# Ten matmuls over zeros behind the weights' transposes of a 3x3 convolution

## The chip, the cores and the metric

The kernel runs on one core of a Trainium2 chip. The metric is the device time of one execution in microseconds (us), the time of the slowest core, and here there is only one. Before the change three runs took 126.99, 127.69 and 127.93 us, median 127.69 us. One more execution was recorded by the hardware profiler; all durations below come from that one.

## The reference

A 3x3 convolution with padding 1 and stride 1, over 16 images with 64 input channels of 64 x 64 and 128 output channels, all in float32:

```
x_pad = np.pad(x, ((0, 0), (0, 0), (1, 1), (1, 1)))
for b, co, ci, kh, kw:
    output[b, co] += weight[co, ci, kh, kw] * x_pad[b, ci, kh:kh+h, kw:kw+w]
```

The input is 16 x 64 x 64 x 64 numbers (16.8 MB), the output 16 x 128 x 64 x 64 (33.6 MB).

## The kernel before

**Arithmetic.** The rows of an output are made in pairs, by a one-dimensional trick in the vertical direction. For output rows 2j and 2j+1 the kernel forms the sum of input rows 2j and 2j+1 (tile `ss`, line 68) and multiplies it by the middle row of weights; this product `U` serves both output rows. The even row is `U` plus a product `A` of two more input rows with the weights G21 and G0, the odd row is `U` plus a product `B` with G01 and G2. G21 and G01 are differences of rows of weights, made on GpSimd (lines 87 and 88). So a block needs 5 products by 3 horizontal taps instead of 6 by 3.

**Tiling.** Two images lie side by side on the 128 partitions (64 channels each). There are 8 such pairs `p`, and each is done in 4 blocks of 8 row pairs. A block issues 30 matmuls on TensorE (line 141): 6 for `U`, 12 for `A`, 12 for `B`. They alternate between the two images, which lie in different halves of the array, so that two of them run side by side; below, "a pair of matmuls" is such a pair. Each has a weight load of its own. The products are accumulated in PSUM, from a pool of 8 banks (`psum`, tag `acc`), and a block takes six of them. ScalarE copies the two `U` tiles out to SBUF (`ut`, line 155); VectorE adds `A` and `ut` (line 165), then `B` and `ut` (line 168), and writes the float32 output tile `ot`.

**Start.** SyncE issues the load of the weights (line 42), of the first pair of images `x0` (line 45) and of the pairs 1 to 3 (`xf`, line 49), all in float32. GpSimd casts the weights to float16 (line 53). TensorE transposes them with 18 matmuls against an identity (line 85), three tiles `wp` of the same PSUM pool, and ScalarE copies these out as `Wt` (line 86). When `x0` has landed, VectorE makes the four pieces of `ss` of pair 0 (line 68) and ScalarE casts `x0` to float16 in four pieces (line 92). The first matmul of line 141 waits for the first of VectorE's pieces. Pairs 4 to 7 come later through GpSimd's queue, cast on the way by the DMA (line 59).

**Stores.** The output of a pair is 4.2 MB in two halves, one for each image: `ots[0]` leaves through SyncE's queue and `ots[1]` through ScalarE's (line 97), both when the fourth block of the pair is done. The last pair is stored in two portions, after its second and its fourth block. Eight buffers are shared by the first loads and the output tiles (`opool`), two of them per pair.

**Order.** Instructions wrapped in `keep` stay in program order on their engine; the others are placed by the framework's scheduler. Each engine runs its own list in order, and waits are semaphores between the lists.

Of the kernel before, what the change touches and what calls it, by code (L numbers as in the profile page):

```python
# [8 lines left out]
F32 = mybir.dt.float32  # L9
F16 = mybir.dt.float16  # L10
# [3 lines left out]
def kernel(  # L14
# [6 lines left out]
    nc = tc.nc  # L21
    B, CI, H, W = x.shape
    CO = weight.shape[0]
# [4 lines left out]
    keep = tc.keep_in_program_order  # L28
# [4 lines left out]
    const = ctx.enter_context(tc.tile_pool(name="const", bufs=1))  # L33
    psum = ctx.enter_context(tc.tile_pool(name="psum", bufs=8, space=bass.MemoryType.PSUM))
# [12 lines left out]
    for p in (1, 2, 3):  # L47
        xf[p] = opool.tile([128, H, W], F32, tag="ot", name="xf")
        nc.sync.dma_start(xf[p], x_rows[128 * p : 128 * p + 128, :, :])
    ident = const.tile([128, 128], F16)  # L50
    make_identity(nc, ident)
    w16 = const.tile([CO, CI * 9], F16)
# [24 lines left out]
    def wrow(i):  # L77
        return Wt[:, i, :, :].rearrange("p t c -> p (t c)")

    for kh, g in ((1, G1), (2, G2), (0, G0)):  # L80
        wp = psum.tile([128, 512], F32, tag="acc", name="wp")
        for k in range(3):
            t = 3 * kh + k
            for q in (0, 64):
                nc.tensor.matmul(wp[q : q + 64, k * CO : k * CO + CO], w16[:, t::9], ident)  # L85
        keep(nc.scalar.copy(wrow(g), wp[:, 0 : 3 * CO]))  # L86
    keep(nc.gpsimd.tensor_sub(wrow(G21), wrow(G2), wrow(G1)))  # L87
    keep(nc.gpsimd.tensor_sub(wrow(G01), wrow(G0), wrow(G1)))  # L88
    load(4)
# [12 lines left out]
    for p in range(NP):  # L102
# [8 lines left out]
        for blk in range(4):  # L111
# [45 lines left out]
            if p + 1 in xf:  # L157
                q = p + 1
# [47 lines left out]
```

## Time and profile before

| what | value |
|---|---|
| median of three runs | 127.69 us |
| the profiled execution | 128.37 us |
| its span, first to last instruction | 126.6 us |
| TensorE busy | 105.8 us (84%), 978 matmuls |
| VectorE, ScalarE, GpSimd busy | 82.7, 52.0, 36.2 us |
| HBM read and written | 17.07 MB and 33.55 MB, 400 GB/s over the span |
| transposes of the weights (line 85) | 4.31 to 5.62 us |
| first and last matmul of line 141 | 9.55 and about 112.8 us |
| last store issued | 115.38 us |

How to read the profile: an engine's busy time says how long its instructions ran, not whether anybody waited for them. The chain of waits goes back from the last computing instruction to what released it, step by step. A transfer is issued by a queue (SPq is SyncE's, ACTq ScalarE's, POOLq GpSimd's) and carried by 16 DMA engines; the "DMA share" of a stretch is the mean busy share of these 16, so 0.50 can mean that eight of them worked all the time; since packets are counted at their start, single short stretches can show a little over 1. "us to landing" counts from the issue of a transfer until the last of the engines is done with it. The column PEclk gives the clock granted to TensorE; the record begins with its first change of state, and before that the column shows 1.00.

The profiled execution took 128.37 us, 1.77 us more than its span (start and end of the program), and 0.68 us more than the median of the runs.

### The profile page before, as it was taken

The page shows a single profiled execution, that of the slowest core. Times are in us where ns is not written, and L with a number is a line of the kernel's source. Part 1 is how long each engine was busy: PE and PEld are TensorE (multiplying, and loading weights), DVE is VectorE, ACT ScalarE, POOL GpSimd, SP SyncE. Part 2 cuts the span into 40 slices and gives each one's busy share as a digit, 9 for nine tenths or more (in the row PEclk, how much of TensorE's full clock was granted, in tenths as well). Part 3 has the DMA queues.
Part 4 walks back from the last instruction along what each step waited for, and adds up shares of the span by engine and source line. Part 5 has one row for each costly group of instructions (what it writes and reads, how often), then busy time and mean ns, then how long its engine had stood idle before and what let it go on. Part 6 is the DMA issues. An engine that isn't in the chain of part 4 may idle for free.

```text
span 126.6 us, 2416 instructions
## 1 busy us (share of the span) xinstructions
PE 105.8 (84%) x978; PEld 57.2 (45%) x978; DVE 82.7 (65%) x132; ACT 52.0 (41%) x84; POOL 36.2 (29%) x27
## 2 busy tenths in 40 slices
PE   0409999999999999999999999999999999990000
PEld 0304455555555555555555555555555555540000
DVE  0025777787778777877777778777877787774000
ACT  4329429933993399333333333333333333330000
POOL 2360093197996000940066000750000000000000
PEclk9999999999999999999999999999999999999855
DMA  6899999999999999999999999999999979999970
GB/s 171 352 456 394 295 306 363 430 440 430 391 324 290 362 396 334 347 321 375 368 352 362 303 409 419 430 419 425 435 430 425 399 316 425 414 438 414 417 324 21
DMA packets 3898, 46.57 MB, mean 368 GB/s; under 512 B 432, under 2 KB 432, under 8 KB 560
## 3 DMA queue, kind: packets, MB, share of 16 engines
q1 hardware_dynamic: 2016, 25.46, 48.2%
q10 hardware_dynamic: 1296, 16.78, 31.5%
q0 software_dynamic: 576, 4.19, 15.8%
q8 instruction: 7, 0.11, 0.3%
q14 instruction: 3, 0.02, 0.0%
HBM read 17.07 MB, written 33.55 MB: 400 GB/s over the span
## 4 chain that ended last, share of the span: by engine, by line
PE 82%; DMA 6%; DVE 2%; issue 1%; DVEq 0%; SPq 0%
PE acc L141 82%; DMA x<-in_x_dram 6%; DVE ot L165 1%; DVE ss L68 1%; DVE ot L168 0%; DVEq L201 0%; SPq L42 0%; DVEq L165 0%
## 5 line engine op out<-in xcount | busy, mean ns | idle before, releaser
L141 PE MATMUL acc<-xs,Wt 64*128 64x504 f16 (+3 forms) x768 | 88.8, 377 | 0.0
L141 PEld LDWEIGHTS <-Wt 64*128 64x128 f16 x960 | 56.1, 95 | 52.0 <-issue 6.0
L165 DVE TENSOR_TENSOR ot<-acc,ut 128x512 f32<-128x512 f32 x64 | 41.2, 686 | 23.8 <-PE acc L141 21.5
L155 ACT COPY ut<-acc 128x512 f32<-128x512 f32 x64 | 34.4, 589 | 54.3 <-issue 34.3
L168 DVE TENSOR_TENSOR ot<-acc,ut 128x512 f32<-128x512 f32 x64 | 41.1, 684 | 0.0
L141 PE MATMUL acc<-ss,Wt 64*128 64x504 f16 (+1 forms) x192 | 27.2, 384 | 3.9 <-DVE ss L68 3.9
L68 POOL TENSOR_TENSOR ss<-xs 128x1024 f16<-128x1024 f16 x8 | 16.8, 2127 | 20.4 <-DMA xs<-in_x_dram 20.4
L68 POOL TENSOR_TENSOR ss<-xf 128x1024 f16<-128x1024 f32 x6 | 14.0, 2355 | 12.5 <-DMA xf<-in_x_dram 12.5
L160 ACT CAST xs<-xf 128x1024 f16<-128x1024 f32 x12 | 12.0, 1057 | 0.0
L68 DVE TENSOR_TENSOR ss<-x 128x512 f16<-128x512 f32 x4 | 2.5, 685 | 8.8 <-DMA x<-in_x_dram 8.8
L59 POOL DMA_DIRECT2D xs<-in_x_dram x4 | 2.4, 601 | 10.4 <-ACT xs L160 10.4
L92 ACT CAST xs<-x 128x1024 f16<-128x1024 f32 (+2 forms) x4 | 3.9, 1042 | 2.6 <-DMA x<-in_x_dram 2.6
L85 PE MATMUL wp<-ident,w 128*64 128x128 f16 x18 | 1.3, 328 | 4.3 <-POOL w L53 4.3
L85 PEld LDWEIGHTS <-w 128*64 128x64 f16 x18 | 1.1, 209 | 4.3 <-POOL w L53 4.3
L86 ACT CAST Wt<-wp 128x384 f16<-128x384 f32 x3 | 1.2, 487 | 3.0 <-PE wp L85 3.0
L86 ACT ACT_TABLE_LOAD x1 | 1.3, 1283 | 0.7 <-PEq L190 0.7
L87 POOL TENSOR_TENSOR Wt<-Wt 128x384 f16<-128x384 f16 x1 | 0.9, 910 | 1.7 <-ACT Wt L86 1.7
L53 POOL CAST w<-w_raw 128x576 f16<-128x576 f32 x1 | 0.7, 664 | 2.3 <-DMA w_raw<-in_weight_dram 2.3
L88 POOL TENSOR_TENSOR Wt<-Wt 128x384 f16<-128x384 f16 x1 | 0.9, 910 | 0.0
masks.py:199 POOL TENSOR_SCALAR_AFFINE_SELECT ident<-ident 128x128 f16<-128x128 f16 x1 | 0.3, 294 | 0.1
masks.py:197 POOL MEMSET ident<- 128x128 f16 x1 | 0.2, 205 | 0.3 <-POOLq L190 0.3
L190 POOL MEMSET const-float32-0.0<- 128x1 f32 x1 | 0.1, 99 | 0.2 <-issue 0.2
(3 smaller groups left out, 0.3 us busy)
## 6 DMA issues: line engine op xcount, KB each, us to landing
out_dram<-ot SPq DMA_DIRECT2D x7, 2048.0 KB, 20.0
out_dram<-ot ACTq DMA_DIRECT2D x7, 2048.0 KB, 19.6
xf<-in_x_dram SPq DMA_DIRECT2D x3, 2048.0 KB, 22.6
xs<-in_x_dram POOLq DMA_DIRECT2D x4, 1024.0 KB, 24.2
x<-in_x_dram SPq DMA_DIRECT2D x1, 2048.0 KB, 7.6
out_dram<-ot SPq DMA_DIRECT2D x2, 1024.0 KB, 11.3
out_dram<-ot ACTq DMA_DIRECT2D x2, 1024.0 KB, 11.2
w_raw<-in_weight_dram SPq DMA_DIRECT2D x1, 288.0 KB, 2.8
```

The source lines that it names most:

```text
L59: keep(nc.gpsimd.dma_start(xs[p], x_rows[128 * p : 128 * p + 128, :, :]))
L68: eng.tensor_add(ss[p][:, lo : lo + n, :], v[:, lo : lo + n, 0, :], v[:, lo : lo + n, 1, :])
L85: nc.tensor.matmul(wp[q : q + 64, k * CO : k * CO + CO], w16[:, t::9], ident)
L86: keep(nc.scalar.copy(wrow(g), wp[:, 0 : 3 * CO]))
L87: keep(nc.gpsimd.tensor_sub(wrow(G21), wrow(G2), wrow(G1)))
L88: keep(nc.gpsimd.tensor_sub(wrow(G01), wrow(G0), wrow(G1)))
L92: keep(nc.scalar.copy(xs[0][:, lo:hi, :], x0[:, lo:hi, :]))
L141: nc.tensor.matmul(tiles[b2][:, lo - j0 : hi - j0, c_lo:c_hi], Wt[p0 : p0 + 64, wi, kw, :], rhs, start=i == 0, stop=i == n - 1,)
L155: keep(nc.scalar.copy(ut, U[b2]))
L160: keep(nc.scalar.copy(xs[q][:, lo : lo + 16, :], xf[q][:, lo : lo + 16, :]))
L165: nc.vector.tensor_add(ots[b2][:, j0 : j0 + RB, 0, :], A[b2], us[b2])
L168: nc.vector.tensor_add(ots[b2][:, j0 : j0 + RB, 1, :], Bt[b2], us[b2])
```

## The change

VectorE first fills a new tile `zeros` (128 x 512, float16) with zeros, and a further tile `warm` is taken from the PSUM pool ahead of the three `wp`. The 18 transposes are now kept in program order, and behind the last of them TensorE runs ten matmuls with 128 columns of `zeros` as weights and all 512 columns as the moving operand, each writing `warm`. Nothing reads `warm`. The first matmul of line 141 comes behind them on TensorE.

```diff
@@ -47,6 +47,14 @@
+    zeros = const.tile([128, 512], F16)
+    keep(nc.vector.memset(zeros, 0.0))
+    warm = psum.tile([128, 512], F32, tag="acc", name="warm")
+
+    def spin(n):
+        for _ in range(n):
+            keep(nc.tensor.matmul(warm, zeros[:, 0:128], zeros))
+
     ident = const.tile([128, 128], F16)
     make_identity(nc, ident)
@@ -82,8 +90,9 @@
             for q in (0, 64):
-                nc.tensor.matmul(wp[q : q + 64, k * CO : k * CO + CO], w16[:, t::9], ident)
+                keep(nc.tensor.matmul(wp[q : q + 64, k * CO : k * CO + CO], w16[:, t::9], ident))
         keep(nc.scalar.copy(wrow(g), wp[:, 0 : 3 * CO]))
+    spin(10)
     keep(nc.gpsimd.tensor_sub(wrow(G21), wrow(G2), wrow(G1)))
```

In the built program the lists of ScalarE, GpSimd and SyncE are the same as before. VectorE's has the memset as a new first instruction. TensorE's has ten weight loads and ten matmuls more, between the transposes and the first matmul of line 141; the first of them waits for the memset. From there on the order on TensorE is that of before, with the PSUM banks shifted by one, so that three of the 192 accumulations of the kernel wait on other semaphores than before; all three lie in the first three blocks.

## The prediction

> **What bounds the kernel now.** I read the chain of waits first. Its pieces in order of time:
>
> ```profile
> 1.17 7.60 DMA x<-in_x_dram
> 9.55 103.26 PE acc L141 x948
> 114.75 0.60 DVE ot L168
> ```
>
> From 9.55 us TensorE runs without a gap to 112.81 us, so it looks like the bound. But this chain stops with VectorE at 115.35 us, and the span is 126.6 us. The last 11 us are transfers, and they have to be read by themselves. The queues on the page:
>
> ```profile
> q1 hardware_dynamic: 2016, 25.46, 48.2%
> q10 hardware_dynamic: 1296, 16.78, 31.5%
> q0 software_dynamic: 576, 4.19, 15.8%
> q8 instruction: 7, 0.11, 0.3%
> ```
>
> The last column adds up to 95.8% of 16 engines' span: 121.3 of 126.6 us. There are 5.3 us in which an average DMA engine did nothing. Where they lie, by stretches of the span (the last two columns are DMA share and GB/s):
>
> ```profile
> 0.00:2.00 2.00, 0.00 (x0) 0.00 (x0) 0.00 (x0) 1.27 (x1) 0.70 (x6) 1.00 0.14 23
> 2.00:101.00 99.00, 92.77 (x858) 50.39 (x860) 71.16 (x114) 46.45 (x76) 35.54 (x21) 1.00 1.01 381
> 101.00:102.50 1.50, 1.50 (x18) 0.81 (x15) 1.50 (x3) 0.60 (x2) 0.00 (x0) 1.00 0.39 164
> 102.50:122.50 20.00, 11.50 (x108) 6.03 (x104) 10.08 (x17) 3.69 (x7) 0.00 (x0) 0.91 0.99 420
> 122.50:125.00 2.50, 0.00 (x0) 0.00 (x0) 0.00 (x0) 0.00 (x0) 0.00 (x0) 0.50 0.14 59
> ```
>
> The DMA engines are full from 2 us to 122.5 us, except for 1.5 us around 101 to 102.5, and there the share is 0.39, not 0: about 6 of 16 worked on. After 122.5 it is 0.14, about 2 of 16. So a few engines lag behind the others, and the end is theirs. Whether the laggards ever run dry is told by the stores. These are the issues of ScalarE's half (column 1 is the time of issue):
>
> ```profile
> 89.77 0.34 ACTq L97 DMA_DIRECT2D out_dram<-ot  x1
> 102.58 0.34 ACTq L97 DMA_DIRECT2D out_dram<-ot  x1
> 108.93 0.34 ACTq L97 DMA_DIRECT2D out_dram<-ot  x1
> 115.38 0.34 ACTq L97 DMA_DIRECT2D out_dram<-ot  x1
> ```
>
> The DMA view, asked for a short stretch around each issue, gives the us to landing for those four in turn:
>
> ```profile
> out_dram<-ot ACTq DMA_DIRECT2D x1, 2048.0 KB, 16.5
> out_dram<-ot ACTq DMA_DIRECT2D x1, 2048.0 KB, 13.6
> out_dram<-ot ACTq DMA_DIRECT2D x1, 1024.0 KB, 12.2
> out_dram<-ot ACTq DMA_DIRECT2D x1, 1024.0 KB, 10.2
> ```
>
> They land at 106.3, 116.2, 121.1 and 125.6 us. The distances are 9.9 us for 4.2 MB (both queues), 4.9 and 4.5 us for 2.1 MB each, while TensorE issued them 12.8, 6.35 and 6.45 us apart. So the last engine ends each store at its own even pace, at 4.9 us per 2.1 MB, and each store is issued long before the one ahead of it has landed (by 3.7, 7.3 and 5.7 us). The earlier ones stand the same way: issued 12.8 us apart, they take 18.5 to 24.5 us to land. **The end of this kernel is set by the DMA engine that lags most, and it has work without a break.** TensorE's end has 5.7 us of cover behind it.
>
> [...]
>
> **The change part by part.** The rows at the start, weight loads of line 141 (start, busy time, count):
>
> ```profile
> 9.93 0.17 PEld L141 LDWEIGHTS <-Wt 64*128 64x128 f16 x2 [0.25 <-issue]
> 10.36 0.18 PEld L141 LDWEIGHTS <-Wt 64*128 64x128 f16 x2 [0.25 <-issue]
> 12.81 0.17 PEld L141 LDWEIGHTS <-Wt 64*128 64x128 f16 x2 [0.20 <-issue]
> 13.18 6.86 PEld L141 LDWEIGHTS <-Wt 64*128 64x128 f16 x64 [0.20 <-issue]
> ```
>
> Up to 13.18 us a pair of matmuls takes 0.43 us at full width (0.375 for the narrower ones); from there 64 loads, 32 pairs, take 6.86 us, 0.214 each. TensorE begins at half pace, and nine pairs take 3.63 us instead of 9 x 0.214 = 1.93: **1.70 us** lost. The granted clock shows 1.00 there, but its record has no entry yet; the pace decides.
>
> *The ten matmuls.* They can begin at 5.62 us (transposes 4.31 plus 1.31). The nearest row is a full-width pair at half pace, 0.43 us: 10 x 0.43 = 4.3 us, end at 9.92, which is **0.37 us** after the 9.55 at which the first real matmul began. Lower end: the pace doubles at once, 10 x 0.214 = 2.1 us, end at 7.8, no delay. Upper end: every load of 128 columns by 128 rows stands beside nothing and costs a transpose's mean of 0.209 on top: 6.4 us, end at 12.0, a delay of 2.45.
>
> *What they gain.* At most the 1.70 us, if the pace is full when the real work begins; at least nothing, if zeros, or this length, do not wake the clock. Before, the pace doubled after 3.6 us of work. From 5.62 that is 9.2, from 4.31 earlier still, so I take all of it: TensorE's work ends 1.70 - 0.37 = 1.33 us earlier. Bounds: 1.70 earlier to 2.45 later.
>
> [...]
>
> *The rest.* The memset lies in VectorE's first 8.80 us, in which it waits for `x0`; behind it only line 68 is queued, and nobody waits unless it took 8 us. Keeping the transposes in order costs nothing, they are in that order already. The shifted banks: block 0 and the next `U` use eight; the next `A` needs the two that ScalarE frees with `ut`, at 12.59 plus 0.53 and 1.06. ScalarE cannot start those earlier, its casts of line 92 run from 8.80 to 12.68. TensorE would reach that `A` at 9.92 + 18 x 0.214 = 13.77, after 13.65: no wait, but that is what is late next, so about 0.1 us of front is left there.
>
> *Where the 1.33 us goes.* All stores are issued 1.33 us earlier. Engines that ran dry near 102 us lose that gap (1.5 us x 0.61 = 0.92 us) and end about 0.9 us earlier. The laggard had no gap: its stores wait 1.33 us longer in the queue and land when they did. Small change: its last 2.1 MB went in 4.5 instead of 4.9 us while the others were out for some 2.8 us; with 0.9 us more of that, 0.4 x 0.9 / 2.8 = 0.13 us. Sum: 128.37 - 0.13 = 128.24 for the profiled execution; that one stands 0.68 over the median, so in runs 127.69 - 0.13 = **127.6 us**. That is no change: about 1% is what a measurement of this kernel can tell from none.
>
> **The rivals.**
> 1. *The lag is not in every execution, the average engine sets the end.* For: the gap at 101 to 102.5 is real, and lag might come and go. Against: eight stores in a row show it. Gain 0.92: 126.8 us.
> 2. *TensorE sets the end after all.* For: it never pauses, and the chain names it. Against: 5.7 us of cover. Gain 1.33 to 1.70: 126.4 to 126.0 us.
> 3. *Slower: the laggard gets one more packet of instructions.* The page shows 7 of them, 0.11 MB, 0.3% of 16 engines' span: 6.1 us, 0.87 us each. If the 20 added instructions push the program over a boundary and the laggard carries the packet: 127.69 + 0.87 = 128.6 us. It decides once the program exceeds what 7 packets and the first fill bring. Against: 20 of 2416 instructions are 0.06 of a packet (0.11 MB / 2416 x 20 = 0.9 KB of 16 KB).
> 4. *It doesn't do what it says*: the clock stays low, the zeros only stand in the way, 0.37 to 2.45 us. All of that lies under the cover, which is at least 10.2 - 7.6 = 2.6 us (a last store of 2.1 MB in both halves against the load of `x0`, the same bytes with almost nothing ahead, 7.6 us): 127.7 us.
>
> **How the numbers follow.** My forecast 0.70 together with rival 4 (both no change, 126.9 to 128.3 by the spread of the runs, 0.94 us, laid around 127.6 and widened to 1.4), rival 1 0.14, rival 2 0.09, rival 3 0.07. Range 126.4 to 128.5: it holds the first two and most of the third, leaves out the lower part of rival 2. Faster by over 1% (under 126.4): rival 2 and a little of 1, 0.10. Slower by over 1% (over 129.0): rival 3 with a bad spread, 0.05. Within 1%: 0.85.
>
> **What would show it.** Right: the slow pairs between 9.9 and 13.2 are gone, the first matmul of line 141 starts at 9.6 to 9.9, the last store is issued near 114 us, the share around 101 us stays near 1, and us to landing of the last stores grows by about 1.3 (10.2 to 11.5) with the span at 126 to 127. Wrong: landing times that do not grow while the issues come earlier (then the engines were not full and rival 1 or 2 holds), or stores that land evenly on all engines.

## The result, and the profile after

The change makes the kernel a little faster: median 126.56 us against 127.93 us, 21 executions each, ratio 0.991 (95% interval 0.989 to 0.994), so 0.9% or about 1.1 us. The ratio, here and below, leaves out executions over 1.5% above the fastest of their kernel, so it can differ from that of the two medians, which are 1.37 us apart here. The forecast was 127.6 us, a gain of 0.13 us. The measured time lies in the range and within the 1% that was called no change, but the gain is eight times the forecast one. It lies between rival 1 (0.92 us) and rival 2 (1.33 us and more), so the size alone does not decide between these.

The start of TensorE's list after the change (start, busy time, count):

```profile
4.30 1.31 PE L93 MATMUL wp<-ident,w 128*64 128x128 f16 x18 [4.30 <-POOL w L61]
5.55 4.44 PE L56 MATMUL warm<-zeros 128*128 128x512 f16 x10
9.92 0.82 PE L150 MATMUL acc<-ss,Wt 64*128 64x512 f16 x6
```

and the weight loads of the real work (line 150 is line 141 of before):

```profile
9.92 9.97 PEld L150 LDWEIGHTS <-Wt 64*128 64x128 f16 x96 [0.83 <-issue]
```

The first real matmul starts at 9.92 us, as worked out (5.62 + 4.3), and the pairs at half pace are gone: 96 loads, 48 pairs, take 9.97 us, 0.208 each, from the first one on. The stores of ScalarE's half, and below them the us to landing of the same four:

```profile
88.34 0.34 ACTq L106 DMA_DIRECT2D out_dram<-ot  x1
101.14 0.34 ACTq L106 DMA_DIRECT2D out_dram<-ot  x1
107.50 0.34 ACTq L106 DMA_DIRECT2D out_dram<-ot  x1
113.95 0.34 ACTq L106 DMA_DIRECT2D out_dram<-ot  x1
```

```profile
out_dram<-ot ACTq DMA_DIRECT2D x1, 2048.0 KB, 15.6
out_dram<-ot ACTq DMA_DIRECT2D x1, 2048.0 KB, 13.5
out_dram<-ot ACTq DMA_DIRECT2D x1, 1024.0 KB, 12.0
out_dram<-ot ACTq DMA_DIRECT2D x1, 1024.0 KB, 9.9
```

All four are issued 1.43 us earlier than before (115.38 to 113.95 for the last), close to the 1.33 of the forecast. But they do not wait longer: 9.9 us instead of 10.2, where 11.5 was forecast. They land at 103.9, 114.6, 119.5 and 123.85 us, the last one 1.75 us earlier than before. The span went from 126.6 to 124.8 us.

Where the DMA engines' time went. These are stretches of the span (last two columns DMA share and GB/s), of the kernel before:

```profile
100.00:106.00 6.00, 6.00 (x60) 3.35 (x58) 5.01 (x8) 2.00 (x4) 0.00 (x0) 1.00 0.85 360
118.00:120.50 2.50, 0.00 (x0) 0.00 (x0) 0.00 (x0) 0.00 (x0) 0.00 (x0) 0.72 1.00 423
120.50:122.00 1.50, 0.00 (x0) 0.00 (x0) 0.00 (x0) 0.00 (x0) 0.00 (x0) 0.50 1.04 437
122.00:125.50 3.50, 0.00 (x0) 0.00 (x0) 0.00 (x0) 0.00 (x0) 0.00 (x0) 0.50 0.21 87
```

and after:

```profile
100.00:106.00 6.00, 6.00 (x60) 2.75 (x58) 4.69 (x8) 2.15 (x4) 0.00 (x0) 1.00 1.01 429
118.00:120.50 2.50, 0.00 (x0) 0.00 (x0) 0.00 (x0) 0.00 (x0) 0.00 (x0) 0.50 1.02 433
120.50:122.00 1.50, 0.00 (x0) 0.00 (x0) 0.00 (x0) 0.00 (x0) 0.00 (x0) 0.50 0.84 355
122.00:125.50 3.50, 0.00 (x0) 0.00 (x0) 0.00 (x0) 0.00 (x0) 0.00 (x0) 0.50 0.09 37
```

The dry stretch at 100 to 106 us is gone: 6 x 0.15 = 0.90 us of an average engine before, nothing after. Beside it, the **idle tail**, what an average engine idles between 118 us and the last landing, has become shorter. Before it is 125.6 - 118 = 7.6 us less the busy 2.5 x 1.00 + 1.5 x 1.04 + 3.5 x 0.21 = 4.8: 2.8 us. After it is 5.85 less 4.13: 1.7 us. Together 2.0 us, against 1.75 of the last landing; the packets themselves took 0.4 us more of an average engine (97.5% of 124.8 us against 95.8% of 126.6), which takes the rest. So two things ended sooner: a common dry stretch, and the lag of the last engines, of which the forecast had said that it would stay. Whether the second belongs to the change is not shown by this: one profiled execution stands on each side, and that of before was a long one (128.37 us).

### The profile page after: what moved, and what is told of

The parts are those of the page before. It is cut to its first block, busy times and chain, and to the rows that moved or that the text cites. A ratio compares the mean times of both kernels' runs of the same rounds, so it can differ in the third digit from the quotient of the medians.

```text
span 124.8 us, 2437 instructions
## 1 busy us (share of the span) xinstructions
PE 108.2 (87%) x988; PEld 49.3 (40%) x988; DVE 82.8 (66%) x133; ACT 52.0 (42%) x84; POOL 36.2 (29%) x27
## 4 chain that ended last, share of the span: by engine, by line
PE 86%; DMA 2%; DVE 1%; issue 1%; POOL 1%; DVEq 0%
PE acc L150 81%; PE warm L56 4%; DMA w_raw<-in_weight_dram 2%; PE wp L93 1%; DVE ot L174 1%; POOL w L61 1%; DVE ot L177 0%; DVEq L210 0%; DVEq L174 0%
## 5 line engine op out<-in xcount | busy, mean ns | idle before, releaser
L150 PE MATMUL acc<-xs,Wt 64*128 64x504 f16 (+3 forms) x768 | 87.0, 373 | 0.0
L150 PEld LDWEIGHTS <-Wt 64*128 64x128 f16 x960 | 46.8, 94 | 56.2 <-issue 0.8
L150 PE MATMUL acc<-ss,Wt 64*128 64x504 f16 (+1 forms) x192 | 26.0, 377 | 0.0
L56 PE MATMUL warm<-zeros 128*128 128x512 f16 x10 | 4.4, 631 | 0.0
L56 PEld LDWEIGHTS <-zeros 128*128 128x128 f16 x10 | 1.3, 143 | 2.3 <-issue 2.2
```

The lines of the kernel that those rows point to most:

```text
L56: keep(nc.tensor.matmul(warm, zeros[:, 0:128], zeros))
L150: nc.tensor.matmul(tiles[b2][:, lo - j0 : hi - j0, c_lo:c_hi], Wt[p0 : p0 + 64, wi, kw, :], rhs, start=i == 0, stop=i == n - 1,)
```

## The experiments

Three theories were on the table. *Laggard* is the forecast: the DMA engine that lags most always has work, so the end does not hear of TensorE. *Gap* is rival 1: only the common dry stretch near 101 us counts. *TensorE* is rival 2. In all tables "late" is TensorE's lateness against the changed kernel.

### Nothing but the frame

```diff
-    spin(10)
+    spin(0)
```

> The change without its ten matmuls: the memset, the tile in PSUM and the fixed order of the transposes stay, no matmul over zeros runs. All theories: the time of before, 127.9 us, within 0.3. They part on the scatter. Laggard (the forecast: the DMA engine that lags most always has work, so the end does not hear of TensorE's start): the time does not depend on when TensorE's clock opens in an execution. Gap (rival 1: all DMA engines together set the end, and only their dry stretch near 101 us can be given or taken by TensorE) and TensorE (rival 2): executions in which the clock opens later end later, by 0.5 us for each us, so over about 1.7 us in all.

Measured 127.26 us, ratio to before 0.999 (0.996 to 1.002). So the memset, the shifted banks and the order of the transposes do nothing that shows, and the gain belongs to the ten matmuls. The scatter is that of before, too: spans of 124.7 to 127.3 us, while 19 of the 21 executions of the changed kernel have spans of 124.4 to 125.1 us (the other two 126.7 and 127.9). In these twelve executions a later opening of TensorE's clock goes with a longer span (correlation 0.81; the opening is estimated as in a later run, below), as gap and TensorE had said and laggard had not. Among the executions of before that ran beside them the correlation is only 0.32 (28 of them, without one of 175.05 us). The profile of this run is of value in itself, as a second look at a kernel with TensorE's start as before, and it has a shorter idle tail:

```profile
100.00:106.00 6.00, 6.00 (x61) 3.28 (x58) 4.95 (x8) 2.13 (x4) 0.00 (x0) 1.00 0.90 374
118.00:120.50 2.50, 0.00 (x0) 0.00 (x0) 0.00 (x0) 0.00 (x0) 0.00 (x0) 0.65 1.01 429
120.50:122.00 1.50, 0.00 (x0) 0.00 (x0) 0.00 (x0) 0.00 (x0) 0.00 (x0) 0.50 1.01 426
122.00:125.50 3.50, 0.00 (x0) 0.00 (x0) 0.00 (x0) 0.00 (x0) 0.00 (x0) 0.50 0.13 54
```

Its last store is issued at 115.26 us, as in before, and lands at 124.3, not 125.6: the idle tail is 6.3 - 4.5 = 1.8 us. The lag on which the forecast was built, 2.8 us, was one execution's. Against this profile the change takes away 0.6 us of dry stretch and only 0.1 us of idle tail.

### Eight, fifteen, twenty, thirty

```diff
-    spin(10)
+    spin(8)      # and 15, 20, 30
```

> Eight matmuls over zeros instead of ten. They end near 9.1 us, ahead of the 9.5 at which the data is there, so the real work starts up to 0.37 us earlier than with ten. Laggard and gap: nothing more to be had, the time of the change, 126.5 us, within 0.2. TensorE: up to 0.37 less, 126.2 us.

> Fifteen matmuls over zeros instead of ten: the five more run at full pace, 5 x 0.214 = 1.07 us, so TensorE and all stores come 1.07 us later than with ten. Theory now: the transfers set a floor near 126.5 us, and lateness of TensorE counts one for one once it exceeds a reserve. Reserve 1.0 us (the best executions of the kernel before, whose TensorE is about 1.05 us later than in the change, are as fast as the change): 126.5 to 126.6 us. Reserve 0.3 us (the run with thirty: 4.0 of 4.28 us arrived): 127.3 us. Laggard: 126.5 us.

> Twenty matmuls over zeros instead of ten: 2.14 us later. Reserve 1.0 us: 127.6 us. Reserve 0.3 us: 128.4 us. Laggard: 126.5 us, as it has cover of 5.5 us.

> Thirty matmuls over zeros instead of ten: at full pace twenty more take 20 x 0.214 = 4.28 us, so all real work on TensorE and all stores come 4.28 us later than with ten. Laggard: the cover is 5.5 us, so 126.6 us, nothing lost. Gap: the share near 101 us was full with ten and about 0.5 us of store were queued in reserve; the rest of the delay is dry time, 126.5 + 4.28 - 0.5 = 130.3 us. TensorE: 126.5 + 4.28 = 130.8 us.

| matmuls over zeros | late, us | median, us | more than with ten | ratio to before |
|---|---|---|---|---|
| 8 | -0.4 | 126.52 | 0.0 | 0.992 |
| 10 | 0 | 126.56 | | 0.991 |
| 15 | 1.07 | 126.85 | 0.3 | 0.995 |
| 20 | 2.14 | 128.28 | 1.7 | 1.006 |
| 30 | 4.28 | 130.51 | 4.0 | 1.023 |

Earlier than with ten brings nothing: that is a floor, and TensorE does not set it. Later costs little at first, then one for one: a reserve of 0.3 to 0.8 us, between the two guesses of the expectation. Laggard is out: with twenty and thirty it said 126.5 and 126.6 us. (Its cover of 5.5 us was that of the last store. At the store of the seventh pair the changed kernel has only 103.9 - 101.14 = 2.8 us, so for thirty it should have said 1.5 us more, about 128.1 us; that is still far from 130.51.) The share at 100 to 106 us falls with the lateness, with fifteen, twenty and thirty:

```profile
100.00:106.00 6.00, 6.00 (x60) 2.83 (x58) 4.69 (x9) 2.15 (x4) 0.00 (x0) 1.00 0.90 380
```

```profile
100.00:106.00 6.00, 6.00 (x60) 2.79 (x58) 4.69 (x8) 2.12 (x4) 0.00 (x0) 1.00 0.87 366
```

```profile
20.00:30.00 10.00, 10.00 (x98) 4.59 (x96) 7.95 (x14) 7.00 (x10) 5.83 (x5) 1.00 0.88 366
...
27.00:28.00 1.00, 1.00 (x14) 0.48 (x10) 1.00 (x3) 0.80 (x2) 1.00 (x1) 1.00 0.50 213
...
100.00:106.00 6.00, 6.00 (x62) 2.77 (x58) 4.70 (x8) 2.15 (x4) 0.00 (x0) 1.00 0.71 298
```

With thirty the engines also run dry near 27 to 28 us, since the first stores of all come only at 28.0 and 28.6 us: a place that nobody had in view. The common dry time explains part of each step, not all. With thirty it is 10 x 0.12 + 6 x 0.29 = 2.9 us of the 4.0 lost, with twenty 6 x 0.13 = 0.8 us of the 1.7. In the profile with twenty the packets also took 0.8 us more of an average engine than after the change (96.5% of 126.9 us against 97.5% of 124.8), and the idle tail is 0.4 us longer.

One thing besides TensorE's lateness differs in these runs. The pages with fifteen, twenty and thirty show one packet of instructions more than the seven of before and of the change:

```profile
q8 instruction: 8, 0.13, 0.4%
```

This is the packet of rival 3. In the traces the eighth comes at about 116 us and takes 0.9 us of one engine. With fifteen the whole loss is 0.3 us (0.5 by the ratios), so there it cost no more than that; with twenty and thirty up to 0.9 us of the loss can be its, and the reserve is uncertain by as much. The late run and twenty with the cut, both below, have eight as well.

### Late at the very end

```diff
+            if p == NP - 1 and blk == 3:
+                late = psum.tile([128, 512], F32, tag="acc", name="late")
+                for _ in range(20):
+                    keep(nc.tensor.matmul(late, zeros[:, 0:128], zeros))
             U = group([(G1, None)])
```

> The change, and twenty more matmuls over zeros ahead of the last block of the last pair of images: 4.28 us on TensorE, late, which delay the last two stores (1 MB each) only. Laggard: the laggard is at the store before until 119.5 us, the last store is issued at 113.95 + 4.28 = 118.2, so 126.6 us, nothing lost. Gap: most engines are done with the store before at about 117.5 us and would wait about 1 us, 127.5 us. TensorE: 130.8 us.

Measured 127.14 us, 0.6 more than the change for 4.28 us of TensorE: between laggard (0) and gap (1.0), and far from TensorE (4.28). The twenty matmuls, the last store and its us to landing:

```profile
109.24 4.49 PE L163 MATMUL late<-zeros 128*128 128x512 f16 x20
```

```profile
118.40 0.34 ACTq L106 DMA_DIRECT2D out_dram<-ot  x1
```

```profile
out_dram<-ot ACTq DMA_DIRECT2D x1, 1024.0 KB, 5.7
```

So a last store with next to nothing ahead of it takes 5.7 us, and the 10.2 us of before held 4.5 us of queue. The cover at the end is real. What has none is lateness that runs through the whole kernel.

### Transfers taken away

In both kernels the stores of the fourth pair of images are left out, 4.2 MB; these two images are not written.

```diff
             parts = {3: (0, 64)} if p < NP - 1 else {1: (0, 32), 3: (32, 64)}
+            if p == 3:
+                parts = {}
```

> The change without the stores of the fourth pair of images (4.2 MB, 9.8 us of all DMA engines; these two images of the output are not written). TensorE's work is untouched. Floor theory: the transfers are then dry ahead of the store at 101.14 us and run from there without a break, 8.4 MB at 428 GB/s, so the time goes down only by what was queued in reserve, 0.3 to 1.0 us: 125.5 to 126.2 us; and the kernel now follows TensorE one for one. TensorE: the same time as the change, 126.5 us.

> The kernel before without the stores of the fourth pair of images (these two images of the output are not written). Floor theory: without a reserve all of TensorE's lateness reaches the end. The clock opens at 12.4 to 15.8 us in this kernel, as far as the executions so far tell, at half pace from 9.55: 1.4 to 3.1 us lost, against 0.37 us of waiting in the change: 1.05 to 2.75 us over the change without these stores, 1.9 us in the mean, 127.4 to 128.1 us. So the gain of the change grows from 1.0 to 1.9 us when transfers are taken away. TensorE: the gain stays as it is, 1.0 us. Laggard: with 9.8 us taken from it, it has no work left over at the end and TensorE decides, as by the floor theory; so this pair does not speak against it, the two runs with fifteen and twenty do.

Measured 125.51 us with the ten matmuls, as the floor theory said, where TensorE had said 126.5. Without them it is 126.70 us, less than the floor theory said: the gain is 1.2 us, hardly more than with all stores. The reason is in the clock. Each execution lists its span and its mean granted clock. The clock falls to half in one step behind TensorE's end (at 119.09 us in the trace of before, where the last matmul ends at about 112.8, and at 115.66 us in that of after, where it ends at about 112.6). If it does so in every execution, the mean tells when: span - 2 x (1 - clock) x span, to some 0.13 us. In the trace of before the record of the clock starts (the clock opens) at 13.27 us, 105.81 us ahead of the fall; after the change at 9.85 us, again 105.81 us ahead of it. With fifteen and with twenty the distance is 109.23 us, with thirty and in the late run 112.64. These differ by 3.42 and 3.41 us, and 31, 32 and 33 times 3.413 us give them. I take it that this step holds in all executions, which these six traces alone do not show; then the fall gives the opening up to a multiple of 3.413. All openings of plain executions in this document are estimates made in this way. I place them in the step from 12.3 to 15.7 us, which holds the openings that traces of kernels without the ten matmuls show (12.96 to 13.42 us); that this is the right place for all is not seen in each execution, but rests on the straight line that comes out. The twelve executions of before without the fourth store give:

```
opens at, us   12.37 12.37 12.46 12.90 13.34 13.34 13.34 14.38 14.57 14.66 14.82 15.63
span, us       124.4 124.4 124.5 124.7 124.9 124.9 124.9 125.3 125.5 125.6 125.5 126.1
```

A straight line of slope 0.49 with a correlation of 0.99: TensorE works at half pace until the clock opens (in the trace of before 0.43 us for a pair of matmuls up to 13.18 us, 0.214 from there), so each us of delay costs half a us, and with 9.8 us of transfers gone all of it reaches the end. The sample had its openings early (median 13.3; in the middle of the step, at 14.0 us, the line gives a span of 125.2 us), whence 126.7. In the six executions with the ten matmuls the spans are 123.2 to 123.7 us, with no such link. At 13.34 the forecast's own sum gives (13.34 - 9.55) / 2 - 0.37 = 1.5 us between the two kernels; the spans differ by 124.9 - 123.45 = 1.45.

The same list for the 29 executions of the complete kernel before that were run beside these has slope 0.40 and a correlation of 0.52; in the sets of 28, 23 and 22 beside the other runs the correlation is 0.32, 0.00 and 0.57. Part of its scatter is the clock, then, and much of it is something else.

The stretch ahead of the seventh pair's store, with and without the ten matmuls, shows DMA engines that stand dry, so that this store's issue sets the rest: from it to the last landing it is 21.2 us in both (100.93 to 122.1 us, 102.66 to 123.9).

```profile
98.00:100.50 2.50, 2.50 (x28) 1.32 (x26) 2.09 (x4) 0.41 (x2) 0.00 (x0) 1.00 0.03 7
```

```profile
100.50:102.50 2.00, 2.00 (x22) 1.15 (x20) 2.00 (x4) 0.51 (x2) 0.00 (x0) 1.00 0.00 0
```

### The dry stretch filled in another way

If the common dry stretch were all, an earlier store could fill it, without any matmul over zeros.

```diff
-            parts = {3: (0, 64)} if p < NP - 1 else {1: (0, 32), 3: (32, 64)}
+            parts = {3: (0, 64)} if p < NP - 2 else {1: (0, 32), 3: (32, 64)}
```

> The kernel before, with the store of the seventh pair of images cut in two portions as that of the last pair is: the first half is issued after the second block, 6.4 us earlier. TensorE's start stays at half pace. Floor theory: the DMA engines have something to do at 101 us whenever the clock opens, so the dry stretch goes without any matmul over zeros, the time is that of the change, 126.4 to 126.6 us, and no longer follows the clock's opening. TensorE and laggard: the time of before, 127.6 us.

> The change, with the same cut of the seventh pair's store. Floor theory: there is no dry stretch left to fill, 126.4 to 126.6 us, the time of the change within 0.2. TensorE: the same, as TensorE does not change.

> Twenty matmuls over zeros and the seventh pair's store in two portions: TensorE as late as in the run with twenty (2.14 us later than in the change), but with early stores for the dry stretch near 103 us, and always in the same state of the clock. Floor theory, pure: the dry stretch goes and nothing else is lost, the time of the change with the cut, 127.0 us. Floor with slow transfers: the run with twenty also moved less at a full share between 30 and 60 us (345 and 338 GB/s there against 376 and 352 in the change), about 1.2 us of transfer, and an earlier store at the end cannot give that back: 128.0 us. TensorE: the time of the run with twenty, 128.3 us, plus the 0.4 of the cut.

> Fifteen matmuls over zeros and the seventh pair's store in two portions, TensorE 1.07 us later than in the change. Floor theory, pure or with slow transfers (the run with fifteen moved 402 GB/s at 20 to 30 us against 379 in the change, and the same after): 126.7 to 127.0 us, no slower than the change with the cut. TensorE: 126.97 plus what fifteen cost without the cut, 0.3: 127.3 us or more.

| kernel, with the cut | median, us | ratio to before | without the cut |
|---|---|---|---|
| before | 128.49 | 1.004 (1.000 to 1.009) | 127.75 |
| ten | 126.97 | 0.997 (0.994 to 1.000) | 126.56 |
| fifteen | 127.44 | 1.003 (0.999 to 1.007) | 126.85 |
| twenty | 128.17 | 1.008 (1.002 to 1.014) | 128.28 |

The cut does fill the stretch, and the time does not come down: for before with the cut the floor theory had said 126.4 to 126.6 us. With fifteen it misses too (127.0 us at most), and the time is what TensorE had said (127.3 or more). Before with the cut, and twenty with the cut:

```profile
100.00:106.00 6.00, 6.00 (x61) 3.24 (x57) 5.01 (x8) 1.91 (x4) 0.00 (x0) 1.00 1.00 419
118.00:120.50 2.50, 0.00 (x0) 0.00 (x0) 0.00 (x0) 0.00 (x0) 0.00 (x0) 0.68 1.02 429
120.50:122.00 1.50, 0.00 (x0) 0.00 (x0) 0.00 (x0) 0.00 (x0) 0.00 (x0) 0.50 0.62 262
122.00:125.50 3.50, 0.00 (x0) 0.00 (x0) 0.00 (x0) 0.00 (x0) 0.00 (x0) 0.50 0.07 28
```

```profile
100.00:106.00 6.00, 6.00 (x60) 2.82 (x58) 4.92 (x8) 1.82 (x5) 0.00 (x0) 1.00 0.98 412
118.00:120.50 2.50, 0.00 (x0) 0.00 (x0) 0.00 (x0) 0.00 (x0) 0.00 (x0) 0.60 0.99 419
120.50:122.00 1.50, 0.00 (x0) 0.00 (x0) 0.00 (x0) 0.00 (x0) 0.00 (x0) 0.50 0.67 284
122.00:125.50 3.50, 0.00 (x0) 0.00 (x0) 0.00 (x0) 0.00 (x0) 0.00 (x0) 0.50 0.06 26
```

The share now falls at 120.5 us, so most engines end sooner. Worked out as above, from the landing of the last store:

| profiled execution | dry at 100 to 106 us | idle tail | last landing |
|---|---|---|---|
| before | 0.9 | 2.8 | 125.6 |
| frame only | 0.6 | 1.8 | 124.3 |
| after | 0 | 1.7 | 123.85 |
| before with the cut | 0 | 2.3 | 124.1 |
| twenty with the cut | 0.1 | 2.9 | 124.6 |
| after with the cut | 0.1 | 1.7 | 123.8 |

Against the profile of frame only, what the cut gives to the average engine comes back as a longer idle tail, and the last landing hardly moves. Against that of before it does not. But the profiled executions of before and of twenty with the cut are faster than their medians (127.06 us against 128.49, 127.65 against 128.17), so these rows cannot tell why the medians stay high.

What the medians do tell: gap, in the form of rival 1, is out as well. With the stretch filled in both kernels the ten matmuls should bring nothing, and they still bring 0.9 us by the ratios, 1.5 us by the medians (128.49 to 126.97). That the kernel before did not become faster by the cut says less, since the cut has a price of its own, 0.4 to 0.7 us with ten. The times of before with the cut do not follow the clock's opening (correlation 0.25), as the floor theory said, but the spans scatter from 125.3 to 128.0 us all the same. The slow transfers that the expectation of twenty with the cut took into account are no better: at 20 to 30 us 423 GB/s were moved there (379 in the change), at 30 to 40 and 40 to 60 us 358 and 343, between twenty without the cut (345 and 338) and the change (376 and 352), and the time is as high. None of these versions is faster than the change.

## Why the prediction was right or wrong

*The start of TensorE* was right in each step: ten matmuls at half pace (4.44 us, forecast 4.3), 0.37 us of delay, no pair at half pace behind them, stores 1.43 us earlier (forecast 1.33). The banks, the memset and the order cost nothing (frame only: ratio 0.999). What the step on the gain passed over is that 1.70 us was the loss of one execution: by the openings estimated above, from 12.4 to 15.6 us, the loss before the change is (12.4 - 9.55) / 2 = 1.4 to (15.6 - 9.55) / 2 = 3.0 us.

*What bounds the kernel* was right in half. TensorE is not the bound in the changed kernel, although it never pauses and the chain of waits names it: 4.28 us on its last block cost 0.6, and 0.4 less at the start brings nothing. The transfers, at a share of 0.99 to 1.02 from 2 to 120.5 us after the change, hold a floor near 126.5 us, and the change brings the kernel to it.

*The step that failed* is "the laggard had no gap: its stores wait 1.33 us longer in the queue and land when they did". They waited 0.3 us less and landed earlier. The forecast had named this as its sign of being wrong: landing times that do not grow while the issues come earlier. That the time lies in its range all the same is luck: the range was wide enough to hold rival 1.

Its first reading, that the engine that ends last works without a break, holds in the profiled executions. The traces keep the landing of each of the sixteen engines for every transfer. Before the change the sixteen landings of the sixth pair's store (ScalarE's half) spread from 101.15 to 106.24 us. Nine of them are ahead of the next issues, at 101.97 (SyncE's half) and 102.58, so those engines ran dry; the last one did not, and the last landing of all, at 125.61, is 19.4 us behind its landing. After the change all lie between 101.98 and 103.97 us (both halves), behind the next issue at 101.14: no engine ran dry, and the last landing of all is 19.9 us behind the last of these. What failed is the second reading, that the lag is the kernel's own and stays:

| profiled execution | next store issued | last landing of the sixth pair | last landing of all |
|---|---|---|---|
| before | 102.58 | 106.24 | 125.61 |
| frame only | 102.45 | 104.74 | 124.27 |
| eight | 100.86 | 104.03 | 123.89 |
| after | 101.14 | 103.97 | 123.82 |
| fifteen | 102.13 | 104.05 | 124.27 |
| twenty | 103.82 | 105.40 | 125.98 |
| thirty | 105.46 | 105.58 | 127.62 |

Before and frame only, with the same start of TensorE, differ by 1.5 us in the third column: the lag differs by execution. And with twenty the sixth pair lands 1.4 us later than with ten, although its last engine still had work when the next store was issued; how much of this is TensorE's lateness and how much the execution's own lag, one execution each does not tell. With thirty 0.1 us of cover is left. The cover was read at the last store (5.7 us forecast, 4.5 by the late run); the smallest, 3.7 us at the seventh pair's store, stood in the forecast's own list.

*The rivals.* Rival 1 gave about the right size, 0.92 us against about 1.1, and the stretch that it named did close. Its reason was not the whole: filling the stretch alone did not bring the gain. Rival 2 was wrong by the floor, though its 1.33 us is about as near to the measured gain. Rival 3 did not occur: the page after the change shows 7 packets of instructions again; its packet came in the runs with fifteen matmuls and more. Rival 4 did not occur.

*What stays open.* That the ten matmuls bring the gain is shown, and that a late TensorE costs a common dry stretch. Later starts cost more than that, and with the stretch filled the gain of the ten matmuls remains. By which way the rest reaches the end, and what makes the sixteen engines end more or less evenly, was not settled: the records give sixteen landings, but not which engine each belongs to.

## What to carry to other kernels

Here, with transfers and TensorE both near the full span, the transfers held a floor near 126.5 us, and an earlier TensorE gained only down to it (126.52 us with eight matmuls, 126.56 with ten). A few runs with a growing delay at the start (0, 1, 2, 4 us) bounded the reserve at 0.3 to 0.8 us, which a profile alone did not give. Such runs change the program's length, so look whether they carry more packets of instructions (here 8 with fifteen, 7 with ten). Cover read at the end of this kernel held for the last transfer, not for lateness that shifts every store: 4.28 us cost 0.6 us on the last block and 4.0 us at the start. And before a lag or a loss is taken from one profile, ask whether it differs by execution, as the idle tail did here (2.8 and 1.8 us with the same start of TensorE): the scatter of the plain times, with the clock of each beside it, tells much of it.

## What the runs showed of the hardware

Matmuls over zeros opened TensorE's clock: at 9.85 us with ten, at 9.04 with eight, ahead of the first real matmul at 9.50, and at 7.71 in the run with the late twenty, there 3.23 us after the first transpose at 4.48 and 2.0 us after the first matmul over zeros at 5.72; without them it opened at 12.96 to 13.42 us in the traces. Whether the transposes count for it was not shown. From opening to fall the profiled executions measured 105.81, 109.23 and 112.64 us. By the openings estimated above, the half pace cost 1.4 to 3.0 us of 127 before the change, or 1.1 to 2.4%, and with 4.2 MB of stores taken away it reached the end in full (0.49 us of span for each us of opening).

In this kernel removing it also removed scatter: with ten 19 of 21 spans lie within 0.7 us, while those of the 29 executions of before beside the runs with fifteen and twenty lie between 124.9 and 127.5 us. Not all of the scatter here is the clock's: with twenty and the cut, where the clock of the profiled execution opened at 9.26 us, 2.5 us ahead of the real work, the spans still lie between 125.4 and 127.3 us. And at a full DMA share the bytes moved differed between versions: 410 GB/s at 20 to 30 us before and 379 after, 372, 376 and 345 at 30 to 40 us before, after and with twenty. What this comes from was not tested.
